# One weight ring for a two-layer decoder trunk: four-block split tiles in one pool, first pair's sums on pages, norm matmuls behind the third product

## The chip, the cores and the metric

The kernel runs on one core of one Trainium2 chip. The metric is the device time of one execution in microseconds (us). Engines are named as in the profile: PE (TensorE, matrix products), DVE (VectorE), ACT (ScalarE), POOL (GpSimd), and SP (SyncE), which here issues every DMA. Each engine runs its own instructions strictly in order, so an instruction that waits holds up all that is queued behind it on that engine.

## What is computed

Two layers of a hybrid decoder trunk are run on 1056 tokens (1024 of a prompt, 8 samples of 4) in fp32. Cut to what matters here, a layer is:

```python
zin = rmsnorm(x, norm_mix_g) @ w_in           # RWKV-7 branch, window attention, two gates
merged = sigmoid(g_r) * (o_r @ w_br_rwkv) + sigmoid(g_a) * (o_a @ w_br_attn)
x = x + merged @ w_out
c, up = split(rmsnorm(x, norm_ffn_g) @ ffn_w_in)     # 1024 -> 2 x 2816
conv = conv_b + sum(c_ext[:, j:j + T] * conv_w[j] for j in range(3))
x = x + (gelu(conv) * up) @ ffn_w_down               # 2816 -> 1024
```

A final rmsnorm is applied to the trunk's output. The change touches how weights are staged everywhere, and the convolutional feed-forward network (FFN) most.

## The kernel before

**Layout and precision.** Activations lie with features on the 128 partitions and tokens along the free axis. Each fp32 operand is split into a rounded high part and the remainder, so one 128x128 weight block costs three matmuls on PE (high by high, high by low, low by high). A weight therefore passes three stages: a DMA brings the raw fp32 tile `wr` (128 x 1024, eight blocks), ACT casts it to the high half `wh`, and DVE or POOL subtracts to give the low half `wl`.

**Weight tiles before.** Outside the FFN, `weights` (L207) stages eight blocks at once: `wr`, `wh` and `wl` are 128 x 1024 each, two buffers of each, in a pool `wts0`/`wts1` that is opened for a layer and closed ahead of its FFN. Inside `ffn` (L1091) there are pools of its own: `rp` with three raw tiles, `hp` with five pairs of four-block tiles `wh`/`wl` (128 x 512) that `split4` (L1102) fills, `fp` for intermediate sums, `zp` for the convolution's input. All of them lie on memory that the stage before (`merge_out`, L1030) has just given back.

**Up-projection.** A pair j is 128 gate rows and 128 up rows; there are 22 pairs a layer. A pair is computed by seven products of half-size operands (Strassen-Winograd): products 1, 2, 6, 5, 7, 4 and 3, each 24 matmuls of 128 x 264. They need sums S1 to S4 of the raw weights (L1182 to L1185, on DVE, from the raw tiles `wg` and `wu`) and sums of the activations, of which operands 1, 2, 6 and 5 are made in `merge_out` and 7, 4 and 3 are brought back from memory as `xh` and split (`operand`, L1117). `keep` copies results u1, u2, u3 out of PSUM; product 1 of pair j+1 (`lead`, L1167) stands ahead of products 4 and 3 of pair j. The norm factor of the FFN's input, `rs`, is not needed by the products; it is multiplied in on POOL afterwards. `rstd` (L261) makes it by a matmul with ones over the sum of squares, a square root on ACT and a reciprocal on DVE, in three column chunks.

**Down-projection.** Three chunks of 352 columns by eight row tiles m by 22 blocks. `chunk` (L1128) brings the activations back (`ar<-ad`), casts and subtracts them. For chunk 0, blocks 0 to 11 are fetched while the last pair of the up-projection still runs. In the last layer, the residual rows `xa` are fetched (L1248) for the final sum.

**Order.** The kernel is written in a tile framework: a scheduler decides at build time in which order each engine's instructions stand, from the program order, the tiles' dependences and how many buffers a pool has. A tile that reuses a buffer waits until the last reader of the tile that was in it is done.

Of the kernel before, what the change touches and what calls it, by code (L numbers as in the profile page):

```python
# [6 lines left out]
F32 = mybir.dt.float32  # L7
F32R = mybir.dt.float32r
# [37 lines left out]
CW = 352  # L46
# [86 lines left out]
class Trunk:  # L133
# [73 lines left out]
    def weights(self, src, k, tag="w", sub=None, pool=None, wr=None, pages=None):  # L207
        nc = self.nc
        wp = pool or self.wp
        if wr is None:  # L210
            wr = wp.tile([128, k, 128], F32, name="wr", tag=tag + "r")
            nc.sync.dma_start(wr if len(src.shape) == 3 else wr.rearrange("p (m k) n -> p m k n", m=src.shape[1]), src)
        if pages is None:
            wh = wp.tile([128, k, 128], F32R, name="wh", tag=tag + "h")
            wl = wp.tile([128, k, 128], F32R, name="wl", tag=tag + "l")
        else:
            wh, wl = (pages.tile([128, T], F32R, name=n, tag="pg")[:, :128 * k].rearrange("p (k n) -> p k n", k=k)
                      for n in ("hi", "lo"))
        nc.scalar.copy(wh, wr)  # L219
        (sub or nc.vector).tensor_tensor(wl, wr, wh.bitcast(F32), ALU.subtract)  # L220
        return wh, wl

# [8 lines left out]
    def dense(self, src, k, rhs, evac, tag="w", sub=None, pool=None, w=None):  # L231
        wh, wl = w or self.weights(src, k, tag, sub, pool)
        pairs = [(wh[:, i], wl[:, i], *rhs[i]) for i in range(k)]
# [135 lines left out]
    def side_work(self, l, xg, rs, pages):  # L369
        nc = self.nc  # L370
        for i in range(22):
            wh, wl = self.weights(self.a["win"][l, 14 + i], 8)
            dst = self.zd[i] if i < 6 else self.td[i - 6]
            for c in range(3):
                s = slice(c * CW, c * CW + CW)
                ps = self.pd.tile([128, CW], F32, name="psg", tag="d")
                for k in range(8):
                    hi, lo = xg[k]
                    nc.tensor.matmul(ps, wh[:, k], hi[:, s], start=k == 0, stop=False)  # L379
                    nc.tensor.matmul(ps, wh[:, k], lo[:, s], start=False, stop=False)  # L380
# [1174 lines left out]
```

## Time and profile before

| | us |
|---|---|
| median of 3 runs | 3501.39 (3487.21 to 3510.01) |
| the profiled execution | 3497.71 |
| its span in the trace | 3495.9 |
| PE busy in it | 3372.5 (96%) |
| mean granted PE clock in it | 0.962 of full |

A timeline row gives the start, the duration, the engine, the line, the operation with what it writes and reads, and in brackets how long the engine was idle just before and what ended that. A row with "x3" joins three such instructions that follow each other. A windows row sums an engine's work in a stretch and gives the granted PE clock there, where 1.00 and 0.50 are 2.4 and 1.2 GHz.

### The profile page before, as it was taken

Reading aid. Unit: us, or ns where it says so; the run is one execution under the profiler, and the core shown is the slowest. Engines: PE = TensorE matmul, PEld = TensorE weight load, DVE = VectorE, ACT = ScalarE, POOL = GpSimd, SP = SyncE. Lnnn points to the kernel's source line nnn. Section 1 sums busy time; section 2 is a strip of 40 time slices with the busy share of each in tenths; the row PEclk is TensorE's granted clock in tenths of the full one; section 3 lists DMA queues with packets and bytes.
Section 4 is the critical chain, followed back from the end, with each engine's and each line's share of the span. In section 5 each row is a group of like instructions: output and inputs, shape, how many; then the busy total and the mean of one; then the engine's idle time right before and its main releaser. Section 6 shows DMA issues by size and latency. Waiting matters only on the chain. (4 is left out here: it accounts for less than half of the span.)

```text
span 3495.9 us, 64743 instructions
## 1 busy us (share of the span) xinstructions
PE 3372.5 (96%) x25078; PEld 3190.0 (91%) x25078; DVE 2249.0 (64%) x4183; ACT 1415.6 (40%) x2700; POOL 1376.8 (39%) x1470
## 2 busy tenths in 40 slices
PE   8999999999989999999999999999999899999998
PEld 7998887888989999999999988878889899999998
DVE  5676676375567777765547767855645777776554
ACT  4442222245334444445534422223543444444443
POOL 5541112132346666633345411222313566665332
PEclk9999888999989999999999989979999899999999
DMA  3335333435642222266623444425264422224664
GB/s 126 106 115 151 99 101 103 142 117 160 208 168 75 79 87 74 92 209 212 194 93 102 135 130 117 110 74 189 89 219 165 142 86 74 74 84 161 204 186 131
DMA packets 299188, 453.32 MB, mean 130 GB/s; under 512 B 85680, under 2 KB 215216, under 8 KB 298592
## 3 DMA queue, kind: packets, MB, share of 16 engines
q1 hardware_dynamic: 297728, 448.92, 40.8%
q8 instruction: 197, 3.23, 0.4%
q14 instruction: 111, 0.91, 0.1%
q10 hardware_dynamic: 1152, 0.26, 0.0%
HBM read 322.58 MB, written 128.53 MB: 129 GB/s over the span
## 5 line engine op out<-in xcount | busy, mean ns | idle before, releaser
L227 PE MATMUL psd<-hi,wh 128*128 128x352 f32 x1248 | 409.6, 329 | 9.2 <-DVE z L286 4.5
L1154 PE MATMUL psA<-x,wh 128*128 128x264 f32 x1408 | 403.7, 287 | 10.9 <-ACT u L1164 8.6
L228 PE MATMUL psd<-lo,wh 128*128 128x352 f32 x1248 | 407.2, 327 | 4.6 <-DVE lo L249 4.6
L1156 PE MATMUL psA<-x,wl 128*128 128x264 f32 x1408 | 403.0, 286 | 8.2 <-DVE wl L1106 8.2
L229 PE MATMUL psd<-hi,wl 128*128 128x352 f32 x1248 | 407.0, 326 | 1.5 <-POOL wl L220 1.5
L1155 PE MATMUL psA<-x,wh 128*128 128x264 f32 x1408 | 403.1, 286 | 0.0
L379 PE MATMUL psg<-hi,wh 128*128 128x352 f32 x1056 | 373.3, 353 | 22.6 <-DVE gt L385 20.8
L1105 ACT CAST wh<-wr 128x512 fp32r<-128x512 f32 (+1 forms) x420 | 246.5, 592 | 302.4 <-PE psd L1281 179.5
L381 PE MATMUL psg<-hi,wl 128*128 128x352 f32 x1056 | 355.3, 336 | 0.0
L380 PE MATMUL psg<-lo,wh 128*128 128x352 f32 x1056 | 354.7, 336 | 0.0
L1280 PE MATMUL psd<-ap,wh 128*128 128x352 f32 x1056 | 342.9, 325 | 5.0 <-ACT wh L1105 4.4
L1281 PE MATMUL psd<-ap,wh 128*128 128x352 f32 x1056 | 342.0, 324 | 2.0 <-DVE ap L1138 2.0
L1282 PE MATMUL psd<-ap,wl 128*128 128x352 f32 x1056 | 341.4, 324 | 0.6 <-DVE wl L1106 0.6
L1106 POOL TENSOR_TENSOR wl<-wr,wh 128x512 fp32r<-128x512 f32 (+1 forms) x196 | 250.0, 1277 | 175.1 <-ACT wh L1105 158.7
L1106 DVE TENSOR_TENSOR wl<-wr,wh 128x512 fp32r<-128x512 f32 (+1 forms) x224 | 168.8, 758 | 190.2 <-ACT wh L1105 189.1
L1154 PEld LDWEIGHTS psA<-x,wh 128*128 128x128 f32 x1408 | 268.1, 190 | 14.3 <-ACT u L1164 9.9
L1156 PEld LDWEIGHTS psA<-x,wl 128*128 128x128 f32 x1408 | 267.7, 190 | 8.9 <-DVE wl L1106 8.9
L1155 PEld LDWEIGHTS psA<-x,wh 128*128 128x128 f32 x1408 | 268.2, 190 | 0.0
L227 PEld LDWEIGHTS psd<-hi,wh 128*128 128x128 f32 x1248 | 236.3, 190 | 14.6 <-ACT wh L219 6.6
L379 PEld LDWEIGHTS psg<-hi,wh 128*128 128x128 f32 x1056 | 207.1, 196 | 44.4 <-DVE gt L385 25.9
L228 PEld LDWEIGHTS psd<-lo,wh 128*128 128x128 f32 x1248 | 236.8, 190 | 7.4 <-DVE lo L249 6.7
L229 PEld LDWEIGHTS psd<-hi,wl 128*128 128x128 f32 x1248 | 236.4, 190 | 2.7 <-POOL wl L220 1.8
(362 smaller groups left out, 8843.4 us busy)
## 6 DMA issues: line engine op xcount, KB each, us to landing
wr<-wdn SPq DMA_DIRECT2D x96, 512.0 KB, 3.7
wr<-wff SPq DMA_DIRECT2D x88, 512.0 KB, 3.5
wr<-win SPq DMA_DIRECT2D x72, 512.0 KB, 4.5
ad<-ct SPq DMA_DIRECT2D x44, 528.0 KB, 2.9
ar<-ad SPq DMA_DIRECT2D x132, 176.0 KB, 3.4
td<-gt SPq DMA_DIRECT2D x96, 176.0 KB, 2.4
gl<-td SPq DMA_DIRECT2D x32, 528.0 KB, 4.7
wr<-wdn SPq DMA_DIRECT2D x40, 384.0 KB, 4.0
```

The lines of the kernel that those rows point to most:

```text
L227: self.nc.tensor.matmul(ps, wh, xh[:, s], start=i == 0, stop=False)
L228: self.nc.tensor.matmul(ps, wh, xl[:, s], start=False, stop=False)
L229: self.nc.tensor.matmul(ps, wl, xh[:, s], start=False, stop=i == last)
L379: nc.tensor.matmul(ps, wh[:, k], hi[:, s], start=k == 0, stop=False)
L380: nc.tensor.matmul(ps, wh[:, k], lo[:, s], start=False, stop=False)
L381: nc.tensor.matmul(ps, wl[:, k], hi[:, s], start=False, stop=k == 7)
L1106: sub.tensor_tensor(lo, x, h.bitcast(F32), ALU.subtract)
L1154: nc.tensor.matmul(ps[c][:, 0:HC], w[0][:, ws], xh, start=first and i == 0, stop=False, skip_group_check=True)
L1155: nc.tensor.matmul(ps[c][:, 0:HC], w[0][:, ws], xl, start=False, stop=False, skip_group_check=True)
L1156: nc.tensor.matmul(ps[c][:, 0:HC], w[1][:, ws], xh, start=False, stop=end and i == 3, skip_group_check=True)
L1280: nc.tensor.matmul(ps, wh[:, ws], hi, start=k == 0, stop=False)
L1281: nc.tensor.matmul(ps, wh[:, ws], lo, start=False, stop=False)
```

## The change

1. One pool `wts` is opened in the setup and kept for the whole kernel: two raw tiles `wr` of 128 x 1024, and four pairs `wh`/`wl` of 128 x 512. Every weight is cast and subtracted in four-block halves, in the FFN too, whose own raw ring (three) and split ring (five) go.
2. For the first pair, S1 to S4 and u1, u2, u3 lie on pages of the large activation pool (tag `pg`), not in `rp` and `fp`.
3. The three norm matmuls are issued behind the last matmul of the first pair's product 6 and write banks of tags A, A and B; before, they wrote tag C. Product 6 is written ahead of the POOL multiplication by `rs`.
4. In the last pair, the fetch of blocks 0 to 11 for the down-projection is written behind the sum that forms `cu`, not ahead of product 6.
5. In the last layer, the eight `xa` loads are issued one by one within the loop over m, not together ahead of it.

```diff
+        _, self.wp = self.pool("wts", bufs=2)            # in the setup; the pools wts0 and wts1 go
...
+    def raw(self, src, k):
+        wr = self.wp.tile([128, 1024], F32, name="wr", tag="wr")
+        self.nc.sync.dma_start(wr.rearrange("p (k n) -> p k n", k=8)[:, 0:k], src)
+        return wr
+
+    def split4(self, x, sub, n=512):
+        wh = self.wp.tile([128, 512], F32R, name="wh", tag="wh", bufs=4)[:, 0:n]
+        wl = self.wp.tile([128, 512], F32R, name="wl", tag="wl", bufs=4)[:, 0:n]
+        self.nc.scalar.copy(wh, x)
+        sub.tensor_tensor(wl, x, wh.bitcast(F32), ALU.subtract)
         return wh, wl
+
+    def weights(self, src, k, sub=None, wr=None):
+        wr = self.raw(src, k) if wr is None else wr
+        ws = []
+        for i in range(0, k, 4):
+            wh, wl = self.split4(wr[:, 128 * i:128 * i + 512], sub or self.nc.vector)
+            ws += [(wh[:, 128 * m:128 * m + 128], wl[:, 128 * m:128 * m + 128]) for m in range(4)]
+        return ws
...
-    def rstd(self, acc, out, cs=range(3), tag="g"):
+    def rstd(self, acc, out, cs=range(3), tags="ggg"):
...
-            ps = (self.pn or self.pg).tile([128, 512], F32, name="psn", tag="n" if self.pn else tag,
-                                           bufs=2 if tag == "C" else None)[:, 0:CW]
+            ps = self.pg.tile([128, 512], F32, name="psn", tag=tags[c], bufs=dict(A=4, B=2).get(tags[c]))[:, 0:CW]
...
-        gs = [self.pool(f"f{n}{l}") for n in "rhuz"]
-        (_, rp), (_, hp), (_, fp), (_, zp) = gs
+        gs = [self.pool(f"f{n}{l}") for n in "ruz"]
+        (_, rp), (_, fp), (_, zp) = gs
+        split4 = self.split4
...
         def fetch(j):
-            raw[j] = [rp.tile([128, 1024], F32, name="wr", tag="wr", bufs=3) for _ in range(2)]
-            for t, i in zip(raw[j], range(2)):
-                nc.sync.dma_start(t.rearrange("p (k n) -> p k n", k=8), a["wff"][l, 2 * j + i])
+            raw[j] = [self.raw(a["wff"][l, 2 * j + i], 8) for i in range(2)]
...
-        def keep(ps, tag):
-            r = [fp.tile([128, HC], F32, name=tag, tag=tag, bufs=2) for _ in range(2)]
+        def keep(ps, tag, j):
+            if j:
+                r = [fp.tile([128, HC], F32, name=tag, tag=tag, bufs=2) for _ in range(2)]
+            else:
+                p = apool.tile([128, T], F32, name=tag, tag="pg")
+                r = [p[:, HC * c:HC * c + HC] for c in range(2)]
...
-            S1, S2, S3, S4 = (rp.tile([128, 512], F32, name=f"s{i}", tag="ws", bufs=4) for i in range(4))
+            if j:
+                S1, S2, S3, S4 = (rp.tile([128, 512], F32, name=f"s{i}", tag="ws", bufs=4) for i in range(4))
+            else:
+                S1, S2, S3, S4 = (p[:, o:o + 512] for p in (apool.tile([128, T], F32, name="ws", tag="pg") for _ in range(2))
+                                  for o in (0, 512))
...
+            product(6, bA, split4(S2, V), False)
             if j == 0:
-                self.pn, self.pg = None, pp
-                self.rstd(rs, rs, tag="C")
+                self.pg = pp
+                with self.tc.issue_after(self.lastP.ins):
+                    self.rstd(rs, rs, tags="AAB")
+            u2 = keep(bA, "u2", j)
             P.tensor_tensor(z[:, 2:2 + HT], z[:, 2:2 + HT], rs[:, h0], ALU.mult)
-            if j == NJ - 1:
-                chunk(0, ao, slots, 0, KE, rp, "ws", 4)
-            product(6, bA, split4(S2, V), False)
-            u2 = keep(bA, "u2")
...
                 V.tensor_tensor(u[:, HT + HC * c:HT + HC * c + HC], bC[c][:, 0:HC], u3[c], ALU.add)
+            if j == NJ - 1:
+                chunk(0, ao, slots, 0, KE, rp, "ws", 4)
...
-                nc.sync.dma_start(xa[m], self.xd[m])
...
-                wr = rp.tile([128, 1024], F32, name="wr", tag="wr", bufs=3)
-                nc.sync.dma_start(wr.rearrange("p (k n) -> p k n", k=8)[:, 0:kn], a["wdn"][l, m, :, k0:k0 + kn])
+                wr = self.raw(a["wdn"][l, m, :, k0:k0 + kn], kn)
...
                 if last:
+                    if c == 0 and m:
+                        nc.sync.dma_start(xa[m], self.xd[m])
...
+                        if last:
+                            nc.sync.dma_start(xa[0], self.xd[0])
                         chunk(0, ao, slots, KE, NJ, rp, "ws", 4)
```

The other lines of the diff pass the list of `(wh, wl)` pairs on to the matmuls that took slices of the full tiles before. PE issues the same matmuls in both kernels.

How the order of the instructions moves is shown at three places. The first is PE at the start of layer 0's FFN, before. `psd<-hi,wl` is the last matmul of `merge_out`; `psn<-rs,con` are the norm matmuls; psA, psB and psC are the banks of products 1 (and 6), 2 and 5.

```order
L229 MATMUL psd<-hi,wl 128x352
L267 MATMUL psn<-rs,con 128x352 [waits DVE_49,Pool_49]
L267 MATMUL psn<-rs,con 128x352 [waits PE_49]
L267 MATMUL psn<-rs,con 128x352 [waits Activation_49]
L1154 MATMUL psA<-x_10215,wh 128x264 [waits Activation_49]
L1155 MATMUL psA<-x_10215,wh 128x264
L1154 MATMUL psA<-x_10215,wh 128x264 [waits DVE_49]
L1155 MATMUL psA<-x_10215,wh 128x264
L1154 MATMUL psB<-x_10219,wh 128x264 [waits Activation_49]
```

PE of the changed kernel at the same place goes from `merge_out` straight into product 1:

```order
L234 MATMUL psd<-hi,wl 128x352
L1149 MATMUL psA<-x_10359,wh 128x264 [waits DVE_49,Activation_49]
L1150 MATMUL psA<-x_10359,wh 128x264
L1151 MATMUL psA<-x_10359,wl 128x264 [waits DVE_49]
L1149 MATMUL psA<-x_10360,wh 128x264
```

and the norm matmuls come behind 91 matmuls of the products, behind product 6 (`psA<-x_10370`) and among the last of product 5 (psC), with product 1 of the second pair after them:

```order
L1150 MATMUL psA<-x_10370,wh 128x264 [waits DVE_49]
L1151 MATMUL psA<-x_10370,wl 128x264
L1150 MATMUL psA<-x_10370,wh 128x264
L1151 MATMUL psA<-x_10370,wl 128x264
L270 MATMUL psn<-rs,con 128x352 [waits Pool_49]
L270 MATMUL psn<-rs,con 128x352
L1150 MATMUL psC<-x_10373,wh 128x264
L1151 MATMUL psC<-x_10373,wl 128x264
L1149 MATMUL psC<-x_10374,wh 128x264
L1150 MATMUL psC<-x_10374,wh 128x264
L1151 MATMUL psC<-x_10374,wl 128x264
L270 MATMUL psn<-rs,con 128x352 [waits DVE_49]
```

The second place is DVE there. Before, the three reciprocals stand ahead of the low halves of the first weights (`wl<-wr`) and of the sums (`wl<-s`):

```order
L1083 TENSOR_TENSOR xs_11011<-xs_11011,xs_10610 128x528 [waits DMAHW4_49,Pool_49]
L1123 TENSOR_TENSOR x_11218<-xh,x_11218 128x528 [waits DMAHW1_49,Activation_49]
L1059 TENSOR_TENSOR x_10226<-xs_10610,x_10226 128x528 [waits Activation_49]
L269 RECIPROCAL rs<-rs 128x352 [waits Activation_49] x3
L1106 TENSOR_TENSOR wl<-wr,wh 128x512 [waits Activation_49]
L1106 TENSOR_TENSOR wl<-wr,wh 128x512 [waits DMAHW2_49,DMAHW3_49,DVE_49,Activation_49]
L1106 TENSOR_TENSOR wl<-s_11092,wh 128x512 [waits Activation_49]
```

In the changed kernel the reciprocals stand behind those low halves and behind the copies out of psB, and ahead of the low halves of operand 7 (`x_11376`, `x_11381`, `x_11386`) and of S1 of the second pair (`s_11585`):

```order
L1194 TENSOR_TENSOR cz<-psB,u_11255 128x264 [waits PE_49]
L272 RECIPROCAL rs<-rs 128x352 [waits Activation_49] x2
L217 TENSOR_TENSOR wl<-ws,wh 128x512 [waits PE_49,Activation_49]
L1118 TENSOR_TENSOR x_11376<-xh,x_11376 128x528 [waits DMAHW3_49,Activation_49]
L272 RECIPROCAL rs<-rs 128x352 [waits Activation_49]
L1118 TENSOR_TENSOR x_11381<-xh,x_11381 128x528 [waits DMAHW4_49,Activation_49]
L1186 TENSOR_TENSOR s_11585<-wr 128x512 [waits DMAHW5_49]
L1118 TENSOR_TENSOR x_11386<-xh,x_11386 128x528 [waits DMAHW6_49,Activation_49]
```

The third place is SP at the start of the last layer's down-projection, before: all eight `xa` loads stand ahead of the weights `wdn`.

```order
L1248 DMA xa_36074<-xd_75 128x1056 [waits DMAHW5_49]
L1248 DMA xa_36076<-xd_76 128x1056 [waits DMAHW6_49]
L1236 DMA o_pconv<-cpo 128x44 [waits DMAHW7_49,Pool_49]
L1248 DMA xa_36078<-xd_77 128x1056 [waits DMAHW0_49,PE_49]
L1237 DMA o_sconv<-cso 128x352 [waits DMAHW1_49,Pool_49]
L1248 DMA xa_36080<-xd_78 128x1056 [waits DMAHW2_49,PE_49]
L1273 DMA wr<-wdn 128x512 [waits DMAHW3_49,DVE_49]
L1273 DMA wr<-wdn 128x1024 [waits DMAHW4_49]
```

In the changed kernel they are mixed, and each weight waits for a split on DVE or POOL to free one of the two raw tiles:

```order
L1298 DMA xa_36399<-xd_77 128x1056 [waits DMAHW3_49,PE_49]
L210 DMA wr<-wdn 128x1024 [waits DMAHW4_49,Pool_49]
L1241 DMA o_pconv<-cpo 128x44 [waits DMAHW5_49,Pool_49]
L1242 DMA o_sconv<-cso 128x352 [waits DMAHW6_49,Pool_49]
L1298 DMA xa_36400<-xd_78 128x1056 [waits DMAHW7_49]
L210 DMA wr<-wdn 128x512 [waits DMAHW0_49,DVE_49]
L1298 DMA xa_36401<-xd_79 128x1056 [waits DMAHW1_49]
L1298 DMA xa_36402<-xd_80 128x1056 [waits DMAHW2_49,PE_49]
```

In the steady part of the up-projection, between the first and the last pair, PE's order is the same in both kernels.

## Rows read from the trace of the kernel before

**Rows 1.** The page: busy time, share of the span and instructions of each engine.
```profile
PE 3372.5 (96%) x25078; PEld 3190.0 (91%) x25078; DVE 2249.0 (64%) x4183; ACT 1415.6 (40%) x2700; POOL 1376.8 (39%) x1470
```

**Rows 2.** Waits of PE: waiting line, what ended it: total us, times, longest.
```profile
PE psn L267 <- POOL rs L259: 13.7, 2, 7.2
PE psA L1154 <- ACT u L1164: 8.6, 5, 3.7
PE psA L1156 <- DVE wl L1106: 8.2, 2, 4.2
...
PE psd L1280 <- ACT wh L1105: 4.4, 1, 4.4
```

**Rows 3.** Windows: stretch, us, busy of PE PEld DVE ACT POOL, clock, DMA share, GB/s.
```profile
1022.30:1047.10 24.80, 11.46 (x39) 8.57 (x40) 21.69 (x18) 13.64 (x22) 11.72 (x11) 0.59 0.65 217
...
2737.20:2763.50 26.30, 12.27 (x41) 9.38 (x42) 22.53 (x19) 13.93 (x23) 12.20 (x11) 0.55 0.66 231
1100.00:1400.00 300.00, 300.00 (x2467) 300.00 (x2466) 217.69 (x280) 130.01 (x260) 188.05 (x173) 1.00 0.24 80
1488.20:1497.00 8.80, 5.22 (x24) 5.20 (x24) 7.93 (x13) 5.73 (x12) 2.19 (x2) 0.61 0.74 232
...
3232.30:3241.20 8.90, 4.51 (x15) 4.28 (x16) 2.74 (x3) 2.28 (x4) 1.28 (x1) 0.62 1.04 399
1761.40:1766.00 4.60, 1.52 (x8) 1.23 (x9) 2.40 (x2) 3.06 (x4) 3.02 (x6) 1.00 0.51 172
```

**Rows 4.** Timeline of PE, start of layer 0's FFN.
```profile
1028.80 2.71 PE L267 MATMUL psn<-rs,con 128*128 128x352 f32 x4 [6.51 <-POOL rs L259]
```

**Rows 5.** Timeline of DVE, end of merge_out and start of layer 0's FFN.
```profile
1013.97 2.87 DVE L1059 TENSOR_TENSOR x<-xs,x 128x528 fp32r<-128x528 f32 x1 [2.74 <-ACT x L1058]
...
1019.13 0.70 DVE L1059 TENSOR_TENSOR x<-xs,x 128x528 fp32r<-128x528 f32 x1
...
1035.36 6.77 DVE L269 RECIPROCAL rs<-rs 128x352 f32<-128x352 f32 x3
```

**Rows 6.** Timeline of POOL, end of merge_out.
```profile
1013.81 2.46 POOL L259 TENSOR_TENSOR rs<-rs,sq 128x1056 f32<-128x1056 f32 x1
```

**Rows 7.** Timeline of several engines in one round of the steady up-projection.
```profile
1219.58 1.31 POOL L1106 TENSOR_TENSOR wl<-wr,wh 128x512 fp32r<-128x512 f32 x1
...
1224.91 0.38 SPq L1114 DMA_DIRECT2D wr<-wff  x1
...
1229.09 2.20 DVE L1182 TENSOR_TENSOR s<-wr 128x512 f32<-128x512 f32 x1 [3.34 <-DMA wr<-wff]
...
1233.00 0.28 PE L1154 MATMUL psA<-x,wh 128*128 128x264 f32 x1
```

**Rows 8.** The page, DMA issues: KB each, median us from issue to landing.
```profile
wr<-wdn SPq DMA_DIRECT2D x96, 512.0 KB, 3.7
```

**Rows 9.** Timeline of ACT, last pair of layer 0.
```profile
1488.99 0.48 ACT L1137 CAST ap<-ar 128x352 fp32r<-128x352 f32 x1 [1.27 <-DMA ar<-ad]
...
1490.01 1.08 ACT L1233 ACTIVATE ct<-ct 128x1056 f32<-128x1056 f32 x1
```

**Rows 10.** Timelines of ACT and POOL, start of layer 1.
```profile
1761.87 1.98 ACT L219 CAST wh<-wr 128x1024 fp32r<-128x1024 f32 x2
...
1762.98 2.36 POOL L220 TENSOR_TENSOR wl<-wr,wh 128x1024 fp32r<-128x1024 f32 x1 [4.94 <-ACT wh L219]
```

**Rows 11.** Timelines of SP and ACT, start of the last layer's down-projection.
```profile
3219.81 2.93 SPq L1248 DMA_DIRECT2D xa<-xd  x6
...
3228.22 2.92 SPq L1273 DMA_DIRECT2D wr<-wdn  x3
...
3236.02 0.62 ACT L1105 CAST wh<-wr 128x512 fp32r<-128x512 f32 x1 [7.20 <-DMA wr<-wdn]
```

**Rows 12.** Groups of instructions by form: form xcount | busy us, mean ns | idle before.
```profile
L219 ACT CAST wh<-wr 128x1024 fp32r<-128x1024 f32 x88 | 91.9, 1046 | 189.9 <-PE psd L228 105.2 <-PE psg L380 70.0 <-DVE xr L1067 7.4
L219 ACT CAST wh<-wr 128x512 fp32r<-128x512 f32 x32 | 19.6, 612 | 23.5 <-PE psd L228 13.0 <-PE psr L402 8.1 <-PE psg L380 2.4
```

More of the change, by code (lines that the diff above doesn't have):

```diff
@@ L229, in mm3, with dense @@
             self.nc.tensor.matmul(ps, wl, xh[:, s], start=False, stop=i == last)
-    def dense(self, src, k, rhs, evac, tag="w", sub=None, pool=None, w=None):
-        wh, wl = w or self.weights(src, k, tag, sub, pool)
-        pairs = [(wh[:, i], wl[:, i], *rhs[i]) for i in range(k)]
+    def dense(self, src, k, rhs, evac, sub=None, w=None):
+        pairs = [(*p, *r) for p, r in zip(w or self.weights(src, k, sub), rhs)]
         for c in range(3):
@@ L371, in side_work @@
         for i in range(22):
-            wh, wl = self.weights(self.a["win"][l, 14 + i], 8)
+            ws = self.weights(self.a["win"][l, 14 + i], 8)
             dst = self.zd[i] if i < 6 else self.td[i - 6]
@@ L391, in side_work @@
         for m in range(8):
-            wh, wl = self.weights(self.a["wbr"][l, m, :, 0:4], 4)
+            ws = self.weights(self.a["wbr"][l, m, :, 0:4], 4)
             for c in range(3):
@@ L400, in side_work @@
                     hi, lo = oo[k]
[L401 to L403 removed]
+                    nc.tensor.matmul(ps, ws[k][0], hi[:, s], start=k == 0, stop=False)
+                    nc.tensor.matmul(ps, ws[k][0], lo[:, s], start=False, stop=False)
+                    nc.tensor.matmul(ps, ws[k][1], hi[:, s], start=False, stop=k == 3)
                     if k == 1:
@@ L1044, in merge_out @@
                 ps = self.pd.tile([128, CW], F32, name="psd", tag="d")
-                self.mm3(ps, [(wh[:, k], wl[:, k], *oo[4 + k]) for k in range(4)], c * CW, CW)
+                self.mm3(ps, [(*ws[k], *oo[4 + k]) for k in range(4)], c * CW, CW)
                 V.scalar_tensor_tensor(gt[1][:, s], gt[1][:, s], 1.0, ps, ALU.add, ALU.mult)
@@ L1155, in product @@
                     nc.tensor.matmul(ps[c][:, 0:HC], w[0][:, ws], xl, start=False, stop=False, skip_group_check=True)
-                    nc.tensor.matmul(ps[c][:, 0:HC], w[1][:, ws], xh, start=False, stop=end and i == 3, skip_group_check=True)
+                    self.lastP = nc.tensor.matmul(ps[c][:, 0:HC], w[1][:, ws], xh, start=False, stop=end and i == 3,
+                                                  skip_group_check=True)
         def bank(tag, bufs):
             return [pp.tile([128, 512], F32, name=f"ps{tag}", tag=tag, bufs=bufs) for _ in range(2)]
-        def keep(ps, tag):
-            r = [fp.tile([128, HC], F32, name=tag, tag=tag, bufs=2) for _ in range(2)]
+        def keep(ps, tag, j):
[4 more added lines that the diff above has]
+                r = [p[:, HC * c:HC * c + HC] for c in range(2)]
             for t, p in zip(r, ps):
@@ L1350, in run @@
                 if c == 0 and k == 1:
-                    wr = self.wp.tile([128, 8, 128], F32, name="wr", tag="wr")
-                    nc.sync.dma_start(wr, a["win"][0, 0])
+                    wr = self.raw(a["win"][0, 0], 8)
                 self.split(pL, "", x, xg[k][0][:, s], xg[k][1][:, s], scale=self.col(0, "gmix", k))
```

39 lines of the change are left out of this document (6 added, 33 removed).

## The prediction

> **What bounds the kernel now.** I read the page's busy times first: PE works 96% of the span and every other engine at most 64% [rows 1]. The matmuls are the same before and after, so the change can only move PE's idle time and the time in which PE runs at half clock. The list of PE's waits came next [rows 2], then windows around the places where the waits lie, to see the clock there [rows 3], then the timelines of the engines that release PE.
>
> The steady part of the up-projection has nothing to win. 2467 matmuls fill 300 us without a gap at clock 1.00 [rows 3], so a matmul of 264 columns costs 300/2467 = 0.1216 us and one pair of 7 x 24 = 168 takes 20.4 us. The losses lie in seams. Largest are the starts of the two FFNs. PE finishes merge_out, then waits 6.5 us in layer 0 for the last addition into the sum of squares on POOL, because the norm matmuls stand ahead of all products [rows 2, 4]. It then runs twelve matmuls on high halves and waits another 4 us for the first low half, which on DVE stands behind three reciprocals of 6.77 us in all [rows 2, 5]. The clock there is 0.59 and 0.55 on average [rows 3]: after the idle time PE is granted 1.2 GHz until it has worked for a while.
>
> What a start costs is the window less its work at full speed. In layer 0's 24.80 us there are 39 records: 33 matmuls of products (33 x 0.1216 = 4.0 us) and six passes of the norm matmuls (2.71 us for four, so 4.1 for six at half clock [rows 4], 2.0 at full). Lost: 24.8 - 6.0 = **18.8 us**. In layer 1's 26.30 us there are 41 records: 35 x 0.1216 = 4.3, and 2.0: lost **20.0 us**. Together 38.8 us, the most that the starts can give.
>
> **The change part by part.**
>
> *Starts of the FFN.* The norm matmuls leave the front of PE's queue; S1 to S4 and u1 to u3 of the first pair, and all weights, no longer wait for memory of merge_out. So product 1 follows merge_out without a wait, and the waits of rows 2 on the sum of squares (13.7 us) and on the low half behind the reciprocals (8.2 us) go. What is late next I replayed by hand: the instructions of each engine in the order of the changed kernel, each with its duration in this trace. The replay keeps PE at full clock and finds stalls in layer 0 at these places:
> - the last low half of operand 2, made from the last row tile of merge_out: 0.4 to 1.8 us;
> - the low half of S2 behind it on DVE: 0.4 to 1.0;
> - weights of the second pair: with four split tiles instead of five, a cast waits until the product four back is done: 1.6 to 2.5 in all;
> - low halves of operand 7: the three reciprocals, 6.77/3 = 2.26 us each [rows 5], now stand between them on DVE: 2 to 3;
> - low halves of S2 and S3 of the second pair, queued on DVE behind operand 7 and slowed by POOL's subtractions for operand 4: 4 to 7.
>
> The near ends sum to about 8.5 us, the far ends to about 15.5. The near end lets DVE and POOL work side by side, the far end lets each wait for the other. The trace speaks for the far end: a DVE subtraction of 128x528 takes 0.70 us alone and 2.87 us when it starts during a POOL addition of 2.46 us [rows 5, 6]. Against it, such meetings are not continuous. The stalls are also split into pieces of 0.4 to 4.5 us. A pause of 3.1 us in two pieces left the clock at 1.00 at the start of layer 1, around a whole one of up to 3.7 us [rows 2] in a last pair it is 0.61 [rows 3], which costs 5.9 us with the pause; so I add 0 to 3 us for the clock and have 8.5 to 18.5 us. I take 13 us lost after the change, just under the middle. Gain: 18.8 - 13 = 6 in layer 0 and 20.0 - 13 = 7 in layer 1, **-13 us**. The bounds are 0 (stalls as large as before) and -38.8.
>
> The Trainium skill, page "SBUF — State Buffer", section "SBUF: two separate sides", says that a DVE operation with two SBUF inputs and a GpSimd operation take a shared port pair as an exclusive lock for the whole instruction, and the other blocks. The pair of 0.70 and 2.87 us agrees with it. By that rule alone the loss would be the 15.5 us of the far end and the gain 38.8 - 31 = 8 us for both starts; it speaks against a full recovery.
>
> *Steady rounds: two raw tiles instead of three, four split tiles instead of five.* Now wu of the next pair can be loaded only when the last split of this pair's wu is done. In before's order that split ends at 1219.58 + 1.31 = 1220.9 [rows 7]. A load needs 1229.09 - 1224.91 = 4.2 us from issue to the sum that waits for it [rows 7], so S1 starts at 1225.1; with S1 2.20, S2 0.7, the cast 0.6 [rows 12] and the low half 0.7, or 2.2 more beside POOL, S2 is ready at 1229.3 to 1231.5, and product 6 starts at 1233.00 [rows 7]. Slack 1.5 to 3.7 us; cost 0. A split now starts three products ahead of its use, 3 x 2.9 = 8.8 us, which covers a cast and a subtraction of 1.3 us with POOL at 63% and DVE at 73% [rows 3]. In the down-projection the same ring holds: 4 blocks are 12 matmuls, about 1.9 us, a raw tile is free about 2 us into the half tile that PE works on, the next lands 3.7 us later [rows 8], and PE needs it six half tiles after, 11.6 us: slack over 3 us with the split. Cost 0.
>
> *Halves instead of full tiles elsewhere.* 88 casts of 1046 ns become 176 of 612 ns [rows 12], 16 us more on an ACT that is busy 40%. DVE and POOL change by less. PE's work hides it; uncovered it would cost up to 16 us over the span, spread thin. Taken 0.
>
> *Start of layer 1.* PE waits for a cast of a full tile (1.98 us for two) and then for the low half on POOL (2.36 us) [rows 10]; the window has 1.52 us of PE work in 4.60 [rows 3], 3.1 lost. With halves the cast is 0.4 us shorter and the subtraction 1.1 us: **-2 us** (0 to -3).
>
> *Last pairs.* PE waits for the copy of u3 [rows 2], which on ACT stands behind casts of 0.48 us and a Gelu of 1.08 us [rows 9]. Moved down, the fetch leaves 8 such casts ahead of that copy in ACT's order instead of 11: 3 x 0.48 = 1.4 us each layer, **-3 us**. The window loses 8.8 - 24 x 0.1216 = 5.9 us [rows 3]; that is the bound, 12 for both. The Gelu stays ahead.
>
> *Last down-projection.* Six xa loads are issued at 3219.81, weights only at 3228.22, and ACT gets them at 3236.02 [rows 11]; the DMA share is 1.04 [rows 3]. PE waits 4.4 us [rows 2] and then works at half clock to 3241.2, 15 records of which about half the 4.5 us is lost: 6.7 us. With the loads mixed, weights come earlier, but the two raw tiles make each wait for a split. **-2 us** (+2 to -6).
>
> **Sum.** -13 - 2 - 3 - 2 = -20 us. Against the profiled execution: 3497.7 - 20 = 3477.7, say 3478. That execution lies 3.7 us under the median of the three runs, whose spread is 23 us; the prediction carries that.
>
> **The rivals.**
> - *Weights late in each round (slower).* If landing, S1, S2 and split take longer than the slack of 1.5 to 3.7 us, PE stops in every round. One microsecond over costs 42 us in 2 x 21 rounds: 3478 + 42 = 3520. For it: the load moves 16 us closer to its use, and S1 already takes 2.20 us beside POOL [rows 7]. Against it: the DMA share is 0.24 [rows 3]. Chance 0.10.
> - *The starts are recovered in full.* If DVE and POOL catch up with product 1 and 2 as cover, 38.8 us go and the other seams 7: 3452. For it: 48 matmuls of cover are 5.8 us that PE never had. Against it: DVE is busy 21.69 of 24.80 us there [rows 3], and this work stays. Chance 0.20.
> - *The stalls only move.* Product 1 starts early, but PE then waits for DVE as long as before; the starts give 0: 3497.7 - 7 = 3491. For it: again DVE's 21.69 us. Against it: the 13.7 us in which PE stood still for POOL [rows 2] now hold work. Chance 0.25.
> - *The forecast*, 0.45.
>
> **How the numbers follow.** The time is the forecast's, 3478. Its own range, from the bounds of the starts (18.5 or 8.5 us lost in each: -2 and -22) and the small seams (+2 to -11 together), runs from 3497.7 - 33 = 3465 to about 3497. The range given, 3450 to 3503, takes in the moved stalls, leaves out late weights (0.10) and cuts the full recovery at its middle (0.10), since with the bounds of the small seams it would fall below 3450: 2 in 10 left out. About 1% is what a measurement of this kernel can tell from no change: 35 us. Faster than 3466: the full recovery and a sliver of the forecast, 0.24. Slower than 3536: late weights by over 1.4 us, with something not seen, 0.09. Within: 0.67.
>
> **What would show it.** PE's waits of the changed kernel: no psn behind the sum of squares, no gap between the last psd and product 1; instead small waits on operands 2 and 7 and on S2 and S3 of the second pair, at clock near 1.00. DVE's reciprocals between halves of operand 7. The steady window still 300 us busy of 300; if PE has a gap there before product 6, the slack was wrong. The copy of u3 in the last pair earlier by over 1 us. If the starts still show half clock for 20 us, stalls have moved, and the prediction is 13 us too low.

## The result and the profile after

The changed kernel takes 3537.33 us (median of 4 runs, 3520.87 to 3547.35); with one more run the kernel before has 3494.47 us (3487.21 to 3510.01). The ratio is 1.0102, with a 95% interval of 1.0071 to 1.0133: slower by 1%, where 0.6% faster was forecast, and outside the range of 3450 to 3503. The profiled execution of the changed kernel took 3536.42 us, so its trace, with a span 38.7 us longer than that of before, is a fair one to compare.

The page's line of busy times answers [rows 1]; columns as there:

```profile
span 3534.6 us, 64936 instructions
...
PE 3399.0 (96%) x25078; PEld 3204.3 (91%) x25078; DVE 2207.1 (62%) x4244; ACT 1431.3 (40%) x2788; POOL 1320.6 (37%) x1497
```

PE's waits of the changed kernel (what waits, what ended it, total us, times, longest) answer [rows 2]:

```profile
PE psd L1283 <- ACT wh L216: 16.7, 11, 6.9
...
PE psA L1149 <- ACT u L1164: 12.3, 5, 3.8
PE psA L1151 <- DVE wl L217: 10.3, 4, 3.4
PE psd L1285 <- DVE wl L217: 7.6, 8, 4.4
...
PE psA L1150 <- DVE x L1118: 4.3, 4, 2.2
```

The 13.7 us behind the sum of squares are gone. In their place stand waits of the down-projection for weights (L1283, L1285), 24.3 us where there were 5.0. In the up-projection the waits for low halves of weights (L1151) are 10.3 us where they were 8.2 [rows 2], and waits for low halves of operands (L1150, 4.3 us) are new.

Windows give the stretches; the columns are those of [rows 3]. First the kernel before: the start of the FFN in either layer (from the last matmul of merge_out to the 505th matmul of the products, which is the start of the fourth pair's share), then its two down-projections:

```profile
1022.28:1104.46 82.18, 68.82 (x512) 65.93 (x511) 66.84 (x72) 41.29 (x77) 46.08 (x40) 0.88 0.39 128
2737.13:2820.59 83.46, 69.36 (x511) 66.47 (x511) 67.69 (x72) 41.77 (x77) 46.95 (x40) 0.86 0.38 129
1499.96:1758.90 258.94, 257.51 (x1592) 256.00 (x1591) 139.35 (x196) 126.26 (x242) 82.70 (x76) 1.00 0.64 197
3216.57:3482.39 265.82, 259.60 (x1592) 257.27 (x1591) 134.20 (x189) 117.44 (x221) 83.51 (x74) 0.99 0.59 185
```

And the same four stretches of the changed kernel, with 300 us of its steady up-projection behind them:

```profile
1023.72:1107.33 83.61, 71.15 (x511) 67.82 (x510) 56.78 (x67) 38.16 (x71) 44.72 (x39) 0.92 0.31 109
2758.87:2840.81 81.94, 70.27 (x510) 67.04 (x510) 58.88 (x66) 38.34 (x71) 43.41 (x39) 0.92 0.31 111
1501.28:1771.70 270.42, 262.20 (x1592) 255.54 (x1591) 140.01 (x199) 127.89 (x250) 87.23 (x77) 1.00 0.63 196
3235.31:3521.17 285.86, 266.96 (x1592) 259.99 (x1591) 130.98 (x192) 116.79 (x225) 83.95 (x75) 0.98 0.56 177
...
1110.00:1410.00 300.00, 300.00 (x2467) 300.00 (x2466) 210.84 (x280) 135.29 (x265) 173.72 (x180) 1.00 0.22 80
```

Cut in this way, by the same PE rows in both traces, the whole span adds up (us, layer 0 and layer 1; the up-projection is cut 400 matmuls before its end, so that the last two pairs and a little more stand by themselves):

| stretch | before | changed | difference |
|---|---|---|---|
| to the first side matmul of layer 0 | 237.8 | 238.8 | +1.1 |
| branches to the end of merge_out | 784.5, 769.4 | 784.9, 780.1 | +0.4, +10.7 |
| start of the FFN | 82.2, 83.5 | 83.6, 81.9 | +1.4, -1.5 |
| steady up-projection | 339.9, 339.4 | 339.8, 339.6 | 0 |
| last pairs | 55.5, 56.6 | 54.1, 54.9 | -1.4, -1.7 |
| down-projection | 258.9, 265.8 | 270.4, 285.9 | +11.5, +20.0 |
| start of layer 1 | 208.8 | 207.1 | -1.8 |
| tail | 13.5 | 13.5 | 0 |

The differences are taken before rounding; their sum is +38.7. The down-projections lost 31.5 us, and the starts, on which the forecast rested, gained nothing. The +10.7 in layer 1's branches is taken up with the last four kernels.

### The profile page after: what moved, and what is told of

It is laid out like the page before. It is cut to its first block, busy times and chain, and to the rows that moved or that the text cites. A ratio compares the mean times of both kernels' runs of the same rounds, so it can differ in the third digit from the quotient of the medians.

```text
span 3534.6 us, 64936 instructions
## 1 busy us (share of the span) xinstructions
PE 3399.0 (96%) x25078; PEld 3204.3 (91%) x25078; DVE 2207.1 (62%) x4244; ACT 1431.3 (40%) x2788; POOL 1320.6 (37%) x1497
## 5 line engine op out<-in xcount | busy, mean ns | idle before, releaser
L216 ACT CAST wh<-wr 128x512 fp32r<-128x512 f32 (+1 forms) x628 | 372.4, 602 | 712.1 <-PE psg L383 171.4
L217 POOL TENSOR_TENSOR wl<-wr,wh 128x512 fp32r<-128x512 f32 (+1 forms) x250 | 344.4, 1379 | 404.7 <-ACT wh L216 392.9
L217 DVE TENSOR_TENSOR wl<-wr,wh 128x512 fp32r<-128x512 f32 (+1 forms) x378 | 280.8, 751 | 338.5 <-ACT wh L216 330.9
L1151 PE MATMUL psA<-x,wl 128*128 128x264 f32 x1408 | 404.1, 288 | 10.3 <-DVE wl L217 10.3
L1150 PE MATMUL psA<-x,wh 128*128 128x264 f32 x1408 | 405.9, 288 | 4.3 <-DVE x L1118 4.3
L1283 PE MATMUL psd<-ap,wh 128*128 128x352 f32 x1056 | 345.6, 328 | 16.8 <-ACT wh L216 16.7
L1285 PE MATMUL psd<-ap,wl 128*128 128x352 f32 x1056 | 345.9, 328 | 9.6 <-DVE wl L217 7.6
L1151 PEld LDWEIGHTS psA<-x,wl 128*128 128x128 f32 x1408 | 269.4, 192 | 11.5 <-DVE wl L217 11.5
L1150 PEld LDWEIGHTS psA<-x,wh 128*128 128x128 f32 x1408 | 269.1, 191 | 5.4 <-DVE x L1118 5.4
```

What stands on the lines that cost most here:

```text
L217: sub.tensor_tensor(wl, x, wh.bitcast(F32), ALU.subtract)
L1150: nc.tensor.matmul(ps[c][:, 0:HC], w[0][:, ws], xl, start=False, stop=False, skip_group_check=True)
L1151: self.lastP = nc.tensor.matmul(ps[c][:, 0:HC], w[1][:, ws], xh, start=False, stop=end and i == 3, skip_group_check=True)
L1283: nc.tensor.matmul(ps, wh[:, ws], hi, start=k == 0, stop=False)
L1285: nc.tensor.matmul(ps, wl[:, ws], hi, start=False, stop=k == NJ - 1)
```

## Experiments: the ring of weight tiles

Where the down-projection loses is seen on ACT, whose casts wait for the weights. The rows are ACT's waits for `wdn` (total us, times, longest), of before and then of the changed kernel:

```profile
ACT wh L1105 <- DMA wr<-wdn: 28.5, 13, 7.2
```
```profile
ACT wh L216 <- DMA wr<-wdn: 131.4, 68, 7.3
```

Three theories were open: two raw tiles are too few there (A), four split pairs are too few (B), the mixed xa loads delay the weights (C). The first kernel gives the down-projection of the changed kernel a third raw tile:

```diff
+        nwr = [0]
...
-                wr = self.raw(a["wdn"][l, m, :, k0:k0 + kn], kn)
+                nwr[0] += 1
+                if nwr[0] % 3:
+                    wr = self.raw(a["wdn"][l, m, :, k0:k0 + kn], kn)
+                else:
+                    wr = rp.tile([128, 1024], F32, name="wr", tag="wr", bufs=1)
+                    nc.sync.dma_start(wr.rearrange("p (k n) -> p k n", k=8)[:, 0:kn], a["wdn"][l, m, :, k0:k0 + kn])
```

> The changed kernel, with a third raw tile for the weights of the down-projection alone (every third load goes to a tile of the FFN's own pool). Theory A (two raw tiles are too few in the down-projection, where a raw tile of two or four blocks takes a whole buffer): the two down-projections lose 12 and 20 us in the changed kernel and get most of it back; about 3537 - 28 = 3509. Theory B (four split tiles instead of five are the cause): unchanged, 3537. Theory C (the order of the xa loads in the last layer): at most a few us of the last down-projection, 3530 to 3537.

Measured: 3508.87 us, ratio to before 1.0001 (0.9972 to 1.0031). Its windows show the two down-projections at 261.80 and 268.36 us, and ACT's waits for the weights are back at the level of before:

```profile
1493.62:1755.42 261.80, 259.50 (x1592) 255.91 (x1591) 141.09 (x199) 129.45 (x250) 89.56 (x77) 1.00 0.66 201
3222.32:3490.68 268.36, 259.93 (x1592) 256.63 (x1591) 132.22 (x193) 119.67 (x228) 84.97 (x75) 0.99 0.60 188
```
```profile
ACT wh L216 <- DMA wr<-wdn: 28.7, 14, 5.2
```

One raw tile gives back 26 of the 31.5 us. The second kernel leaves two raw tiles and adds a fifth split pair:

```diff
-        split4 = self.split4
+        nsp = [0]
+
+        def split4(x, sub, n=512):
+            nsp[0] += 1
+            if nsp[0] % 5:
+                return self.split4(x, sub, n)
+            wh = rp.tile([128, 512], F32R, name="wh", tag="wh", bufs=1)[:, 0:n]
+            wl = rp.tile([128, 512], F32R, name="wl", tag="wl", bufs=1)[:, 0:n]
...
```

> The changed kernel, with a fifth pair of split tiles inside the FFN (every fifth split goes to tiles of the FFN's own pool); two raw tiles stay. Theory A (raw tiles): unchanged in the down-projections, 3530 to 3537, and a few us at most at the starts of the FFN, where a cast waited for the product four back. Theory B (split tiles): both down-projections recover, about 3507.

Measured: 3512.09 us, ratio 1.0026 (1.0000 to 1.0052). The down-projections take 268.4 and 274.1 us: -2.0 and -11.7 against the changed kernel. That is neither theory in its pure form. Layer 0 stays with theory A; in layer 1 the fifth pair takes over half of the loss, and ACT still waits long for the weights (148.8 us in 82 times and 43.3 us in 21, at its two lines). By the code the two rings work in series: a raw tile comes free when its last half is split, and a half is split when a split pair is free, so either ring being longer lets the loads start earlier. The median fell by more than the 14 us of these stretches. The branches of its profiled execution were 17.6 us shorter than those of the changed kernel; how much they vary is treated below.

The third kernel issues the xa loads ahead of the loop again:

```diff
                 xa.append(apool.tile([128, T], F32, name=f"xa{m}", tag="pg"))
+                nc.sync.dma_start(xa[m], self.xd[m])
...
-                    if c == 0 and m:
-                        nc.sync.dma_start(xa[m], self.xd[m])
...
-                        if last:
-                            nc.sync.dma_start(xa[0], self.xd[0])
```

> The changed kernel, with the eight xa loads of the last layer issued together ahead of the down-projection, as before the change. Theory A: the last down-projection still lacks raw tiles; within 5 us of 3537, its first wait longer. Theory C (mixed xa loads delay the weights): the last down-projection gets back most of its 20 us, about 3520; that of layer 0 is unchanged at +12.

Measured: 3531.81 us, ratio 1.0093 (1.0057 to 1.0129); the last down-projection takes 288.5 us, 2.6 more. Theory C falls: mixing the loads costs nothing here. The fourth goes the other way, with one number changed in the kernel before (at both places where the FFN takes raw tiles):

```diff
-                wr = rp.tile([128, 1024], F32, name="wr", tag="wr", bufs=3)
+                wr = rp.tile([128, 1024], F32, name="wr", tag="wr", bufs=2)
```

> The kernel before with one edit: two raw tiles instead of three in the FFN, for the up- and the down-projection. Theory A: both down-projections slow by 10 to 20 us each, the steady up-projection does not; about 3494 + 28 = 3522. Theory B and C: unchanged, 3494. Late weights in each round, as feared in the prediction, would show as a gap in each of 42 rounds, 3536 or more.

Measured: 3524.22 us, ratio 1.0055 (1.0027 to 1.0082). Two raw tiles by themselves make the kernel before slower; its down-projections take 270.2 and 277.6 us (+11.3 and +11.8), and the steady up-projection 340.0 and 339.4, as before. Taking the two edits on the ring together:

> The changed kernel, with a third raw tile in the down-projection and a fifth pair of split tiles in the FFN. If the ring of weight tiles is the whole cause of the loss, both down-projections return to the 258.9 and 265.8 us of before, where the third raw tile alone left 261.8 and 268.4, and the small gains of the other seams stay (last pairs -3, start of layer 1 -3): about 5 us under the kernel before, 3489 to 3500. If something else of the change costs time (halves of weights outside the FFN), it stays 5 to 15 us above before.

Measured: 3495.52 us, ratio 0.9980 (0.9965 to 0.9995). The down-projections are at 258.68 and 260.79 us:

```profile
1508.48:1767.16 258.68, 257.76 (x1592) 255.91 (x1591) 140.14 (x196) 127.97 (x246) 85.12 (x76) 1.00 0.66 200
3225.14:3485.93 260.79, 257.69 (x1592) 255.26 (x1591) 134.63 (x190) 117.28 (x221) 84.45 (x74) 1.00 0.61 190
```

Both down-projections together take 556.3 us with two raw tiles and four split pairs (the change), 530.2 with three and four, 542.5 with two and five, 519.5 with three and five, and 524.8 in the kernel before. The loss of the change is the two rings in the down-projection, the raw ring more than the split ring.

The last down-projection is now 5 us under before. In this kernel and in the three further ones below with the same rings it takes 260.6 to 262.3 us, against 265.8 and 265.7 in the two kernels that have the rings of before and all xa loads ahead. The mixed xa loads are the likely reason, but the fetch for the last pair was moved too, and the two were not tried apart.

Where in the down-projection the time is lost, windows tell. In chunk 0 the first four of the eight row tiles are fetched in small pieces, first 8 + 4 blocks of each, then 8 + 2 of each; the other four row tiles and chunks 1 and 2 are fetched as 8 + 8 + 6. Layer 0, the small pieces and then all the rest, of before and of the changed kernel:

```profile
1500.08:1542.59 42.51, 42.51 (x267) 42.51 (x266) 27.56 (x37) 20.30 (x39) 14.63 (x13) 1.00 0.66 207
1542.59:1758.90 216.31, 214.88 (x1326) 213.37 (x1326) 111.67 (x160) 105.89 (x203) 67.95 (x64) 1.00 0.64 195
```
```profile
1501.40:1552.53 51.13, 45.58 (x266) 42.02 (x264) 26.60 (x38) 21.25 (x42) 16.91 (x14) 1.00 0.62 199
1552.53:1771.70 219.17, 216.50 (x1325) 213.40 (x1326) 113.30 (x161) 106.58 (x208) 70.20 (x63) 1.00 0.63 196
```

A sixth of the matmuls takes 8.6 of the 11.5 us lost. In layer 1 it is 11.9 of 20.0, and in the kernel before with two raw tiles 21.5 of the 23.1 us of both layers. Outside the small pieces layer 1 loses 8.1 us only where both rings are short, one wait of 4.4 us for a low half among it; with a third raw tile or a fifth split pair that part is 1.2 us or less.

## Experiments: the start of the FFN

In the changed kernel product 1 starts without a wait, as intended, yet the start is as long as before. PE's timeline there, rows with idle time ahead of them:

```profile
1032.48 0.39 PE L1151 MATMUL psA<-x,wl 128*128 128x264 f32 x1 [1.98 <-DVE wl L217]
...
1051.74 0.39 PE L1150 MATMUL psA<-x,wh 128*128 128x264 f32 x1 [1.71 <-DVE x L1118]
...
1055.59 0.39 PE L1149 MATMUL psA<-x,wh 128*128 128x264 f32 x1 [0.92 <-ACT wh L216]
1059.77 0.59 PE L1151 MATMUL psA<-x,wl 128*128 128x264 f32 x1 [3.42 <-DVE wl L217]
```

A later one, of 2.21 us for the copy u on ACT, is at 1070.65. The wait of 3.42 us is for the low half of S2 of the second pair. On DVE one follows its queue backwards (the first row is of earlier work and is used further below):

```profile
1027.76 2.96 DVE L1189 TENSOR_TENSOR ws<-wr,ws 128x512 f32<-128x512 f32 x1
...
1041.41 4.56 DVE L272 RECIPROCAL rs<-rs 128x352 f32<-128x352 f32 x2 [2.45 <-ACT rs L271]
1045.89 1.22 DVE L217 TENSOR_TENSOR wl<-ws,wh 128x512 fp32r<-128x512 f32 x1
1047.04 1.62 DVE L1118 TENSOR_TENSOR x<-xh,x 128x528 fp32r<-128x528 f32 x1
1048.58 2.34 DVE L272 RECIPROCAL rs<-rs 128x352 f32<-128x352 f32 x1
...
1054.73 1.61 DVE L1188 TENSOR_TENSOR s<-wr 128x512 f32<-128x512 f32 x1
1056.26 1.78 DVE L1189 TENSOR_TENSOR s<-wr,s 128x512 f32<-128x512 f32 x1
1057.97 1.74 DVE L217 TENSOR_TENSOR wl<-s,wh 128x512 fp32r<-128x512 f32 x1
```

DVE works without a pause from 1041.4 to 1059.7, and 6.9 us of it are the reciprocals. Just ahead of them it stood still for 2.45 us. So theory D: DVE's queue bounds the start, and the norm matmuls behind product 6 put the reciprocals where DVE is already late. The rival, E: loads or the ring of four bound it. The first test takes the reciprocals out:

```diff
-            nc.vector.reciprocal(out[:, s], out[:, s])
```

> The changed kernel without the three reciprocals of the FFN's norm factor in each layer (the factor is left as the square root, so part of the computation is left out). Theory D (DVE's queue bounds the start of the FFN: the reciprocals, 2.3 us each, stand ahead of the low halves that the second pair needs): from the end of merge_out to the fourth pair 83.6 and 81.9 us become about 76, 6 to 8 us less in each layer, and the half clock there goes or halves. Theory E (loads, or the ring of four split tiles, bound the start): within 2 us of 83.6 and 81.9.

Measured, one execution, of which only the stretch counts: 75.68 and 76.84 us. That is 7.9 and 5.1 us less, close to what D says and far from E. The granted clock of the stretch rises from 0.92 to 0.95 and 0.93, so in layer 1 the half clock went down by less than was expected. How far such a stretch varies by itself is seen in three kernels whose start is that of the change (itself, with the third raw tile, with the xa loads ahead): 80.2 to 83.8 us. The starts of the kernel before, as it is, with two raw tiles and with halves alone, take 82.2 to 84.7 us. The second test moves the norm matmuls back:

```diff
...
-            product(6, bA, split4(S2, V), False)
             if j == 0:
                 self.pg = pp
-                with self.tc.issue_after(self.lastP.ins):
-                    self.rstd(rs, rs, tags="AAB")
-            u2 = keep(bA, "u2", j)
+                self.rstd(rs, rs, tags="CCC")
             P.tensor_tensor(z[:, 2:2 + HT], z[:, 2:2 + HT], rs[:, h0], ALU.mult)
+            product(6, bA, split4(S2, V), False)
+            u2 = keep(bA, "u2", j)
```

> The changed kernel with the norm matmuls written and issued as before the change (bank C, ahead of product 6), all else as changed. If moving them was what took the old waits away, PE waits again for the sum of squares on POOL, and the start is longer than 83.6 and 81.9 us by 3 to 7 us. If DVE's queue is the bound either way, the start stays within 2 us.

Measured, one execution: 78.11 and 77.05 us, 5 us *less* each, against both expectations on record. The scheduler did not put them back at the front: with the rest of the change in place they come during product 6, early enough that the reciprocals fill time in which DVE had nothing to do. Its DVE rows:

```profile
1030.73 0.70 DVE L1062 TENSOR_TENSOR x<-xs,x 128x528 fp32r<-128x528 f32 x1
1031.35 4.55 DVE L272 RECIPROCAL rs<-rs 128x352 f32<-128x352 f32 x2
...
1036.44 2.34 DVE L272 RECIPROCAL rs<-rs 128x352 f32<-128x352 f32 x1
...
1047.04 0.68 DVE L217 TENSOR_TENSOR wl<-s,wh 128x512 fp32r<-128x512 f32 x1
```

Merge_out ends at 1020.2 here and at 1023.7 in the changed kernel. The first reciprocal thus starts 11.1 us after it, not 17.7, and the low half of S2 of the second pair starts after 26.8 us, not 34.3. The expectation had taken over PE's place of the norm matmuls from the kernel before, where memory of merge_out, too, held the products back. The third test undoes the pages:

```diff
-            if j:
+            if True:
                 S1, S2, S3, S4 = (rp.tile([128, 512], F32, name=f"s{i}", tag="ws", bufs=4) for i in range(4))
...
-            if j:
+            if True:
                 r = [fp.tile([128, HC], F32, name=tag, tag=tag, bufs=2) for _ in range(2)]
```

> The changed kernel with the first pair's sums S1 to S4 and the copies u1 to u3 in the FFN's own pools again, which lie on memory of merge_out. If the pages are needed to start early, PE waits after product 1 or 2 for about 3 to 6 us, since S1 to S4 can be formed only when the last row tile of merge_out is done; the start becomes 86 us or more. If they are not, within 2 us of 83.6 and 81.9.

Measured, one execution: 75.98 and 76.24 us. The waits after product 1 that were expected are there (PE stands still 3.4 us within product 2 and 6.3 us before product 6 in layer 0), and the start is shorter by 7.6 and 5.7 us all the same, since hardly any wait follows. This too was against what was written. The windows of layer 0, cut 22.5 us behind the end of merge_out, show why, without the pages and then in the changed kernel:

```profile
1016.68:1039.20 22.52, 12.81 (x83) 11.76 (x82) 16.46 (x18) 12.29 (x23) 14.09 (x12) 0.77 0.64 214
1039.20:1092.66 53.46, 52.57 (x431) 52.25 (x430) 41.40 (x50) 25.59 (x51) 31.14 (x28) 1.00 0.22 75
```
```profile
1023.72:1046.30 22.58, 19.40 (x132) 17.77 (x131) 15.84 (x16) 13.52 (x25) 10.34 (x10) 0.92 0.54 186
1046.30:1107.33 61.03, 51.75 (x379) 50.04 (x379) 40.94 (x52) 24.64 (x47) 34.38 (x30) 0.92 0.22 80
```

PE waits nearly as long in both, 10.6 us without the pages and 12.5 with them. Without them the waiting lies at the front, and much of the half clock falls into it; behind it PE runs at 1.00 with 0.9 us of waiting. With them it comes in many pieces up to 1070.65, the clock is 0.92 throughout, and the same matmuls keep PE busy for 71.2 us in place of 65.4. So 5.8 of the 7.6 us are busy time, matmuls at the lower clock above all.

## Experiments: what beats both kernels

Three of the last four combine edits already shown. First the two ring edits with the norm matmuls of the second test above:

> The changed kernel with the third raw tile in the down-projection, the fifth pair of split tiles, and the norm matmuls issued as before the change. Theory D (DVE's queue bounds the start; norm matmuls behind product 6 put the reciprocals where the second pair's low halves are due): the starts fall from 81.0 and 80.9 us to about 76, 5 us less each, and the time to about 3486, 0.4% under the kernel before. If the gain seen without these rings does not add to theirs, 3495.

Measured: 3479.69 us, ratio 0.9935 (0.9908 to 0.9962). Its starts take 78.25 and 77.73 us, where about 76 was expected, its down-projections 260.10 and 260.55:

```profile
1021.95:1100.20 78.25, 68.64 (x512) 66.09 (x510) 58.09 (x69) 39.09 (x73) 44.97 (x39) 0.93 0.36 123
2731.72:2809.45 77.73, 69.48 (x510) 66.71 (x510) 56.65 (x70) 39.46 (x74) 44.69 (x39) 0.93 0.36 124
1493.92:1754.02 260.10, 258.56 (x1592) 255.80 (x1591) 141.32 (x197) 128.15 (x246) 84.60 (x76) 1.00 0.65 199
3202.84:3463.39 260.55, 257.87 (x1592) 255.25 (x1591) 134.21 (x189) 117.20 (x221) 84.22 (x74) 1.00 0.61 190
```

Next the ring edits with the pages undone:

> The changed kernel with the third raw tile in the down-projection and the fifth pair of split tiles, and the first pair's sums S1 to S4 and u1 to u3 in the FFN's own pools again. Theory D: the one longer pause at the front lets DVE do the reciprocals while PE waits, and no short stalls follow; starts of 74 to 77 us, time about 3485. If the pages help once the split ring has five tiles, 81 us or more.

Measured: 3484.89 us, ratio 0.9945 (0.9919 to 0.9971); starts 78.5 and 76.9 us, in layer 0 above the 74 to 77 expected. And with both undone:

> The changed kernel with the third raw tile and the fifth split pair, norm matmuls as before the change, and the first pair's sums in the FFN's own pools. Of the change there remain the one pool for the weights outside the FFN, the fetch for the last pair, and the xa loads. Theory D: starts of 75 to 78 us, no better than either edit alone, about 3486. If only the edit that keeps PE from the front wait counts, the waits of the kernel before return here, 82 and 83 us, about 3497.

Measured: 3486.46 us, ratio 0.9960 (0.9930 to 0.9989). The starts are 83.3 and 83.7 us, as the second branch of the expectation had it, though the time is that of the first. The waits are not those of before: the norm matmuls come behind product 2, the three reciprocals stand ahead of the sums S1 to S4 on DVE, and PE waits 9.3 us in one piece in each layer for the cast of S2. The intervals of the last three ratios overlap, so the medians do not tell which of the three is best; the starts are read from one trace each. By these, either of the two edits alone is worth 5 to 7 us a layer at the start, and both together, as in the change, only 2 to 3 (81.0 and 80.9 us with the same ring edits). The fourth is the kernel before with nothing but halves of weights outside the FFN (the functions `raw`, `split4` and `weights` of the change, in the pools of each layer):

> The kernel before with one edit: weights outside the FFN are cast and subtracted in four-block halves, two raw tiles and four split pairs a layer's pool; the FFN keeps its own rings. Theory F (halves cost time in the branches, where the stretch from the first side matmul to the end of merge_out took 780.1 us in layer 1 against 769.4): 5 to 15 us more than before, 3500 to 3515. If that difference was chance (that stretch holds 78 to 147 us of half clock in the runs so far, unlike from run to run): within 5 us of before, less 3 us for layer 1's start.

Measured: 3505.16 us, ratio 1.0014 (0.9978 to 1.0050). The interval reaches from 8 us less to 18 us more, so it does not rule out theory F's 5 to 15 us. The traces say more. The branches of its profiled execution took 803.1 and 778.6 us, but PE's idle time in them, where a late half would show, is 49.4 us where it was 46.1 before. Of the +10.7 us of layer 1's branches in the changed kernel's trace, 1.1 us is idle time (23.1 against 22.0), and the other 9.6 us are the same matmuls at a lower mean clock (0.94 against 0.95). So halves cost at most about 3 us of waiting, and the rest is within what this stretch does from run to run.

## Why the prediction was wrong, step by step

**The step that failed most: the shorter rings in the down-projection, "slack over 3 us", cost 0.** The two rings cost 31.5 us in the changed kernel; two raw tiles alone cost the kernel before 23.1. The working counted raw tiles of eight blocks, which last PE 3.9 us. But the first four row tiles of chunk 0 come in pieces of 8, 4, 8 and 2 blocks, and a piece of two or four blocks takes a whole buffer: 16 pieces in 42.5 us of work are 2.7 us of PE a buffer. A buffer's round there was 6.4 us (16 pieces in 51.1 us, two buffers; a load of 3.9 us, the page's median for eight blocks, a cast and a subtraction are 5.2 of it), more than the 5.3 us of work in two buffers. Three buffers hold 8.0 us of work, and pieces of 8 + 8 + 6 blocks 7.1 us in two buffers; both keep up, or nearly so, in the windows above. What the forecast called unlikely for the up-projection (weights late in each round, 0.10, the one rival on the slower side) happened, at another place than the rival named. The steady up-projection itself, for which a slack of 1.5 to 3.7 us was worked out, came out as forecast: 300 us busy of 300.

**The starts, -13 us: measured 0.** The old waits did go, and most of the new stalls stood where the list put them. What failed is the term for the clock, "0 to 3 us". 504 matmuls and the norm passes are 63.3 us of work, so the changed kernel loses 83.6 - 63.3 = 20.3 and 18.6 us where 13 was taken. PE's idle time is 12.5 and 11.7 us of that (83.61 - 71.15 and 81.94 - 70.27 in the windows above), the middle of the 8.5 to 15.5 of the replay. The other 7.9 and 7.0 us are busy time beyond the 63.3, matmuls at the lower clock above all, at a mean clock of 0.92. In the kernel before that part was 5.5 and 6.1 us, although its mean clock was lower (0.88 and 0.86), because much of the half clock fell into waiting. The forecast let this part fall where it rose. The rival "the stalls only move" (0.25) described the starts.

The rule of the Trainium skill's page "SBUF — State Buffer", section "SBUF: two separate sides", cited in the prediction for the far end of the replay, is seen at work: the subtraction that forms S4 took 2.96 us in the row above of 1027.76, beside POOL, where those of 128 x 512 elsewhere take 0.68. The waiting did not reach that far end. The reciprocals' place, which the working had seen and priced at 2 to 3 us, cost more: the two experiments took 5 to 8 us off a start by it, 3 to 5 of them idle time of PE and the rest busy time. The other 12 to 15 us of a start's loss were not taken apart, beyond what the test of the pages shows.

**Last pairs, -3 us: -1.4 and -1.7, for another reason.** PE's wait for u3 did not shorten (3.59 us in layer 0, 3.58 before), because ACT still runs the Gelu just ahead of the copy; the casts that left its queue had stood in time when ACT was waiting:

```profile
1490.99 0.49 ACT L1132 CAST ap<-ar 128x352 fp32r<-128x352 f32 x1 [2.34 <-DMA ar<-ad]
1491.39 0.61 ACT L216 CAST wh<-wr 128x512 fp32r<-128x512 f32 x1
1492.07 1.08 ACT L1238 ACTIVATE ct<-ct 128x1056 f32<-128x1056 f32 x1
1493.08 0.48 ACT L1132 CAST ap<-ar 128x352 fp32r<-128x352 f32 x1
1493.47 0.37 ACT L1164 COPY u<-psA 128x264 f32<-128x264 f32 x1
```

What was gained is half-clock time: 3.4 us of it in place of 6.8. That it is chance is likely: two of the other kernels with this edit show 6.8 us there again, and the two experiments on the kernel before, without it, show 3.4 or none.

**Start of layer 1, -2 us:** -1.8, and -3.3 to -3.6 in most of the other kernels with halves; in the kernel with halves alone +0.3, though PE's idle time there fell from 4.8 to 3.6 us. **Halves, 0:** about 3 us of waiting at most, as shown above. **Last down-projection's start, -2 us (+2 to -6):** PE's first wait there grew from 4.4 to 6.9 us in the changed kernel; with longer rings the whole stretch is 3.5 to 5 us shorter than before.

## What to carry to other kernels

Count buffers in a ring for the stretch where the tiles are smallest, not for the usual tile: the time that one buffer's content keeps the engine busy there, times the number of buffers, must exceed a buffer's whole round of load, cast and subtraction. When a wait on the critical engine is removed, look next at the engine that fed it: if that queue has no spare time, a long instruction moved later on it comes out as new waits, and the place where the queue stood idle is where it belongs. Price a stall with the clock it leaves behind: here short waits spread over 40 us cost more than two pauses at the front of nearly the same length.

## What the runs showed of the hardware

The branches, which no edit but the one pool with its halves touches, took from 1547 us (both layers together) to 1582 us in the fourteen profiles, and that goes with the granted clock. The windows of layer 0's branches in two kernels that are the same up to there show it: 0.96 and 0.92 of full clock for the same matmuls, 766.81 and 794.48 us.

```profile
239.76:1006.57 766.81, 745.20 (x5839) 673.13 (x5838) 480.95 (x1147) 272.71 (x543) 187.98 (x180) 0.96 0.46 140
```
```profile
239.17:1033.65 794.48, 773.45 (x5839) 697.19 (x5838) 476.93 (x1147) 272.20 (x542) 186.28 (x180) 0.92 0.44 135
```

A difference of 10 us in this kernel can thus not be read from two traces; it needs the stretch in which the edit acts, or many runs. What makes the clock fall more often in one execution than in another was not tried.
